# New priorities and re-measured costs in the list scheduler of a one-core encoder layer

## The chip, the core and the metric

The kernel runs on one core of one Trainium2 chip. The metric is the device time of one execution in microseconds (us); less is better. A core has five engines that run on their own and meet at semaphores: PE (TensorE, matrix products), DVE (VectorE), ACT (ScalarE), POOL (GpSimd) and SP (SyncE, which here only issues transfers). Each engine works off its own list of instructions strictly in the order in which the list was written: an instruction that has to wait holds up everything behind it on that engine.

## What is computed

The reference is one layer of a streaming encoder for 512 prompt frames and 32 sample frames (544 columns in all), cut here to its steps:

```python
xn = RMSNorm(x);  [q|k|v|iq|ik|iw|u|g_a|g_b] = xn @ w_in
score = sum_h iw[t,h] * relu(iq[t,h] . ik[s]);  top_idx = top_k(score, n_sel)
o_A = softmax(q . k[top_idx]) @ v[top_idx]          # sparse attention, GQA
m = u + (u_prev - u) * shift_mu                     # RWKV-7 branch, from u
S = S * w_t + (S @ a_t) b_t + v_t k_t;  y_t = S @ r_t
h = x + w_out(sigmoid(g_a) * (o_A @ w_oa) + sigmoid(g_b) * (y_B @ w_ob))
y = RMSNorm_final(h + SwiGLU(RMSNorm(h)))
```

All of it is in float32. A float32 product is done as three PE passes over operands that are split into a high and a low part.

## The kernel before

**Products.** `gemm` (line 279) multiplies one 128-column block of weights by the activations, in two halves of 272 columns, each in a PSUM bank of its own: 8 slices of the contraction by 3 passes are 24 matmuls per bank. Its weights come through `wblock`: a transfer (line 255) into `raw`, a rounding copy on ACT (line 256, the high part), a subtraction on DVE (line 260, the low part).

**The start.** `prologue` loads the input in eight slices (line 296, each 128x544), the first two blocks of w_x, small vectors and constants. Line 300 (ACT) and 301 (DVE) split every slice into `x0`, which the listings call `k`: x times the norm's gain, not yet divided by the root mean square. Three blocks are multiplied from `x0` directly (two of the low-rank part, group L, in banks 82 to 85, and the first block of group U0, in banks 86 and 89), 3 x 48 = 144 matmuls; line 758 scales their results afterwards. Meanwhile the sum of squares is made: lines 309, 311 (squares and sums), 316, 317 (twenty small matmuls), 318, 319, 322, then five transposes on PE (line 328), two copies on ACT (line 330), and from them, slice by slice, the normalised input `xn` (the listings' `r`): line 339 on DVE, 340 on ACT, 341 on DVE, eight times each. The next two blocks of U0 are multiplied from `xn` (2 x 48 = 96 matmuls), then line 392 makes keys and values. Lines 439 and 424, 425 load and split the first cached index keys, which nothing needs before the index scores much later.

**After that** the branches run interleaved: the index scores and the top-k search on DVE (lines 458, 459, 530, 604 to 616), attention, four pairs of RWKV heads with their preparation (lines 901 to 1045) and a recurrent chain of nine steps each (lines 1058, 1061, 1064 on PE, with copies on DVE, ACT and POOL between), the gates and the merge, all with blocks of line 279 between them as filler. From about 514 us on, gates, output projection and feed-forward are an unbroken sequence of large products (lines 279 and 1330).

**What sets the order.** The program is written once in the order of the string `ORDER`, whose words are groups (L, U0, KV, P0 ...). `plan` (line 1602) gives each instruction a priority: the one from the place where it is written, plus `SHIFT[group]`; the smaller goes first. `S` is the group of the sums of squares and of `xn`; a `w` ahead of a name means the group's weight blocks. `schedule` (line 1654) then walks through a model of the engines in time: whenever an engine is free it takes the ready instruction with the smallest priority. The model uses a duration per instruction (`cost`), a delay between engines (`HOP`), an extra for a change between partition halves (`TURN`) and a time for each transfer. Its only result is the order on each engine, which the program is then built with; nothing of the model's times goes to the chip.

## Time and profile before

| quantity | value |
|---|---|
| median of 3 runs | 1007.6 us (1006.28 to 1008.33) |
| the profiled execution, its own time | 1007.89 us |
| span of the profiled execution, first to last instruction | 1006.1 us |
| PE busy / DVE busy / ACT busy / POOL busy in the span | 964.9 / 628.1 / 460.0 / 190.4 us |
| mean granted TensorE clock | 0.985 |

The span leaves out 1.8 us of the profiled execution's own time that lie around it. A busy share is an average over stages with very different limits, so the rows further down split the span into stages.

### The profile page before, as it was taken

Reading aid. Unit: us, or ns where it says so; the run is one execution under the profiler, and the core shown is the slowest. Engines: PE = TensorE matmul, PEld = TensorE weight load, DVE = VectorE, ACT = ScalarE, POOL = GpSimd, SP = SyncE. Lnnn points to the kernel's source line nnn. Section 1 sums busy time; section 2 is a strip of 40 time slices with the busy share of each in tenths; the row PEclk is TensorE's granted clock in tenths of the full one; section 3 lists DMA queues with packets and bytes.
Section 4 is the critical chain, followed back from the end, with each engine's and each line's share of the span. In section 5 each row is a group of like instructions: output and inputs, shape, how many; then the busy total and the mean of one; then the engine's idle time right before and its main releaser. Section 6 shows DMA issues by size and latency. Waiting matters only on the chain.

```text
span 1006.1 us, 20829 instructions
## 1 busy us (share of the span) xinstructions
PE 964.9 (96%) x8268; PEld 923.4 (92%) x8268; DVE 628.1 (62%) x1452; ACT 460.0 (46%) x965; POOL 190.4 (19%) x307
## 2 busy tenths in 40 slices
PE   6989999999989999999999999999999999999996
PEld 5979997898879887899899999999999999999995
DVE  5947635999999898799677654444444444313132
ACT  6644555465546876565734452222323222223231
POOL 2212213322423421220000231111111111011112
PEclk9999999899999998999999999999999999999998
DMA  6246332432343455343555322232222233223222
GB/s 229 84 119 193 113 101 64 126 115 88 122 133 106 144 172 142 120 129 94 153 154 188 122 84 85 87 99 89 84 85 84 85 89 95 72 87 96 79 74 89
DMA packets 63282, 112.58 MB, mean 112 GB/s; under 512 B 13616, under 2 KB 33872, under 8 KB 63056
## 3 DMA queue, kind: packets, MB, share of 16 engines
q1 hardware_dynamic: 62144, 110.72, 35.7%
q8 instruction: 65, 1.06, 0.5%
q10 hardware_dynamic: 1040, 0.52, 0.2%
q14 instruction: 33, 0.27, 0.1%
HBM read 93.67 MB, written 17.14 MB: 110 GB/s over the span
## 4 chain that ended last, share of the span: by engine, by line
PE 72%; DVE 14%; DMA 6%; ACT 4%; issue 2%; SPq 1%; POOL 0%; DVEq 0%; ACTq 0%; POOLq 0%
PE bank L279 49%; PE bank L1330 13%; PE bank L458 1%; DVE w L260 1%; DVE f L616 1%; PE bank L459 1%; DMA iq_dram<-f 1%; DMA raw<-in_w_x_dram 1%; DVE f L611 1%; DVE f L615 1%; PE bank L901 1%; DVE f L529 1%; ACT w L256 1%; PE bank L1058 1%; DVE f L928 1%
## 5 line engine op out<-in xcount | busy, mean ns | idle before, releaser
L279 PE MATMUL bank<-r,w 128*128 128x272 f32 x4752 | 658.3, 293 | 3.2 <-ACT f L762 2.8
L279 PEld LDWEIGHTS bank<-r,w 128*128 128x128 f32 x4752 | 617.3, 189 | 10.0 <-ACT f L762 3.5
L256 ACT ACTIVATE w<-raw 128x1024 fp32r<-128x1024 f32 (+1 forms) x135 | 137.8, 1021 | 223.6 <-PE bank L279 172.7
L260 DVE TENSOR_TENSOR w<-raw,w 128x1024 fp32r<-128x1024 f32 (+1 forms) x135 | 176.5, 1308 | 97.8 <-ACT w L256 97.6
L1330 PE MATMUL bank<-r,w 128*128 128x272 f32 x1056 | 133.0, 288 | 0.0
L1330 PEld LDWEIGHTS bank<-r,w 128*128 128x128 f32 x1056 | 132.4, 188 | 0.0
L1308 POOL TENSOR_TENSOR f<-f 128x544 f32<-128x544 f32 x22 | 30.4, 1382 | 234.0 <-DVE f L1305 224.9
L1305 DVE TENSOR_TENSOR f<-bank,f 128x272 f32<-128x272 f32 x44 | 19.4, 442 | 74.8 <-PE bank L279 74.8
L1298 DVE TENSOR_TENSOR f<-bank,f 128x272 f32<-128x272 f32 x44 | 19.1, 435 | 45.1 <-PE bank L279 45.1
L453 POOL TENSOR_TENSOR k<-f,k 64x512 fp32r<-64x512 f32 (+1 forms) x22 | 30.1, 1372 | 49.0 <-ACT k L452 43.4
L458 PE MATMUL bank<-k 128*128 128x512 f32 (+5 forms) x102 | 35.8, 359 | 3.1 <-DVE f L645 1.3
L1332 DVE TENSOR_TENSOR f<-bank,f 128x272 f32<-128x272 f32 x16 | 7.1, 442 | 47.7 <-PE bank L1330 47.7
L1336 POOL TENSOR_TENSOR f<-f 128x272 f32<-128x272 f32 x13 | 12.4, 955 | 110.8 <-ACT f L1334 110.8
L459 PE MATMUL bank<-k 128*128 128x512 f32 (+5 forms) x102 | 33.0, 333 | 0.0
L1334 ACT ACTIVATE f<-f 128x272 f32<-128x272 f32 x16 | 6.8, 423 | 57.1 <-DVE f L1332 57.1
L1299 ACT ACTIVATE f<-f 128x272 f32<-128x272 f32 x44 | 18.7, 424 | 29.8 <-DVE f L1298 29.8
L611 DVE SCALAR_TENSOR_TENSOR f<-f,f 128x256 f32<-128x256 f32 (+2 forms) x45 | 31.7, 705 | 0.9 <-ACT f L604 0.3
L279 PE MATMUL bank<-k,w 128*128 128x272 f32 x144 | 22.8, 322 | 9.8 <-ACT k L300 9.8
L279 PEld LDWEIGHTS bank<-k,w 128*128 128x128 f32 x144 | 21.6, 219 | 10.1 <-ACT k L300 9.7
L458 PEld LDWEIGHTS bank<-k 128*128 128x128 f32 x102 | 19.1, 188 | 10.7 <-issue 5.1
L1074 POOL COPY f<-f 64x64 f32<-64x64 f32 x56 | 16.3, 292 | 65.3 <-DVE f L1071 63.9
L1250 POOL TENSOR_TENSOR f<-f 128x272 f32<-128x272 f32 x14 | 12.5, 896 | 75.3 <-DMA raw<-in_w_out_dram 51.7
(352 smaller groups left out, 1239.0 us busy)
## 6 DMA issues: line engine op xcount, KB each, us to landing
raw<-in_w_x_dram SPq DMA_DIRECT2D x41, 512.0 KB, 3.7
raw<-in_w_gate_dram SPq DMA_DIRECT2D x22, 512.0 KB, 3.6
raw<-in_w_up_dram SPq DMA_DIRECT2D x22, 512.0 KB, 3.6
raw<-in_w_down_dram SPq DMA_DIRECT2D x16, 512.0 KB, 3.6
gate_dram<-f SPq DMA_DIRECT2D x16, 272.0 KB, 2.4
raw<-in_w_oa_dram SPq DMA_DIRECT2D x8, 512.0 KB, 3.8
raw<-in_w_out_dram SPq DMA_DIRECT2D x8, 512.0 KB, 3.7
f<-iq_dram SPq DMA_DIRECT2D x26, 128.0 KB, 2.8
```

The source lines that it names most:

```text
L256: nc.scalar.activation(hi[:, a], raw[:, a], AF.Copy)
L260: self.lo_eng.tensor_tensor(lo[:, b], raw[:, b], hif[:, b], op=OP.subtract)
L279: nc.tensor.matmul(o, a[:, k], c[k][:, s], start=n == 0, stop=n == 3 * nk - 1)
L453: nc.gpsimd.tensor_tensor(ql[0:64], raw[0:64], qh_r.v(512)[0:64, :n], op=OP.subtract)
L458: nc.tensor.matmul(out, q[0][:, i:i + m], self.KS[:, j, keys], start=True, stop=False)
L459: nc.tensor.matmul(out, q[1][:, i:i + m], self.KS[:, j, keys], start=False, stop=stop)
L611: nc.vector.scalar_tensor_tensor(acc, r[:, i * S:(i + 1) * S], w, acc, op0=OP.mult, op1=OP.add)
L1298: nc.vector.tensor_tensor(t1[:, s], o, self.rs[:, s], op=OP.mult)
L1299: nc.scalar.activation(t1[:, s], t1[:, s], AF.Silu)
L1305: nc.vector.tensor_tensor(t2[:, s], o, self.rs[:, s], op=OP.mult)
L1308: nc.gpsimd.tensor_tensor(t1, t1, t2, op=OP.mult)
L1330: nc.tensor.matmul(o, a[:, k], c[k0 + k][:, s], start=m == 0, stop=m == 65)
```

## The change

The instructions stay the same, with the same operands and buffers (7,429 matmuls in both). What changes is the model and the table that decide the order. The delay from POOL to ACT goes from 250 to 112 ns and from POOL to DVE from 70 to 110 ns; ACT's turn goes from 128 to 132 ns. A transfer now occupies the queue of SP for 330 ns, or 585 ns where it covers fewer than 128 partitions (the new `narrow`), instead of 60 ns; its way through the queue is counted from that. All entries of `SHIFT` have new values.

```diff
 SHIFT = {
...
-    "R0": 299400, "R1": -1861400, "R2": -142400, "R3": 126400, "S": -59800, "SI": 126900, "U0": -21700, "U1": 1680300, "U2":
...
+    "R0": 156800, "R1": -241500, "R2": 188700, "R3": 345300, "S": -198800, "SI": -132300, "U0": -640200, "U1": 1595200,
...
-       ("Activation", "DVE"): 142, ("DVE", "Activation"): 128, ("DVE", "Pool"): 155, ("Activation", "Pool"): 210, ("Pool", "Activation"): 250,
-       ("Pool", "DVE"): 70, ("DVE", "DVE"): 127, ("Pool", "Pool"): 104, ("Activation", "Activation"): 60, ("PE", "PE"): 0}
+       ("Activation", "DVE"): 142, ("DVE", "Activation"): 128, ("DVE", "Pool"): 155, ("Activation", "Pool"): 210, ("Pool", "Activation"): 112,
+       ("Pool", "DVE"): 110, ("DVE", "DVE"): 127, ("Pool", "Pool"): 104, ("Activation", "Activation"): 60, ("PE", "PE"): 0}
...
-TURN = {"Activation": 128, "DVE": 110, "Pool": 112}
+TURN = {"Activation": 132, "DVE": 110, "Pool": 112}
...
+def narrow(i):
+
+    return any(list(x.ap)[0][1] < 128 for x in list(i.outs) + list(i.ins) if hasattr(x, "ap"))
...
-    sides = [0 if x or e in ("PE", "SP") else side(i) for x, e, i in zip(dma, engine, L)]
+    sides = [32 * narrow(i) if x else 0 if e == "PE" else side(i) for x, e, i in zip(dma, engine, L)]
...
                 if dma[k]:
-                    queue = max(t0 + 67, queue + 25) + 450
+                    issue = 585 if sides[k] else 330
+                    queue = max(t0 + 67, queue) + issue + 120
                     bus = max(queue + 650, bus) + work[k]
-                    end, free[e] = bus, t0 + 60
+                    end, free[e] = bus, t0 + (issue if e == "SP" else 60)
```

The order that comes out differs on every engine up to the long sequence of large products, and hardly in that sequence. Three places follow. In the listings a number behind `x` counts equal instructions in a row, and 128x272 is the size of the result.

**The first transfers**, on SP, in its queue's order from the first instruction. Before:

```order
L255 DMA raw<-in_w_x_dram 128x1024
L439 DMA f_74<-in_cache_keys_dram 128x512 x2
L225 DMA f_58<-in_vec_dram 128x80
L255 DMA raw<-in_w_x_dram 128x512
L296 DMA f_58<-in_x_t_dram 128x544 x4
L298 DMA f_58<-in_consts_dram 128x494
L255 DMA raw<-in_w_x_dram 128x512
L296 DMA f_58<-in_x_t_dram 128x544 x4
```

The same of the changed kernel:

```order
L255 DMA raw<-in_w_x_dram 128x1024
L225 DMA f_58<-in_vec_dram 128x80
L255 DMA raw<-in_w_x_dram 128x512
L296 DMA f_58<-in_x_t_dram 128x544 x4
L298 DMA f_58<-in_consts_dram 128x494
L255 DMA raw<-in_w_x_dram 128x512
L296 DMA f_58<-in_x_t_dram 128x544 x4
L439 DMA f_74<-in_cache_keys_dram 128x512 x2
```

The two transfers of cached keys (line 439) go from behind the first weight block to behind all eight slices of the input (line 296).

**The products around the transposes**, on PE, from the last small matmuls of the sum of squares on; `k` is `x0`, `r` is `xn`. Before:

```order
L279 MATMUL bank_83<-k,w 128x272 x5
L328 MATMUL bank_88<-f_58 128x32
L328 MATMUL bank_88<-f_58 128x128 x2
L328 MATMUL bank_87<-f_58 128x128 x2
L279 MATMUL bank_86<-k,w 128x272 x22
L279 MATMUL bank_89<-k,w 128x272 x22
L279 MATMUL bank_83<-k,w 128x272 x4
L279 MATMUL bank_84<-k,w 128x272 x11
L279 MATMUL bank_82<-r_70,w 128x272 x2
L279 MATMUL bank_85<-k,w 128x272 x14
L279 MATMUL bank_82<-r_70,w 128x272 x16
L279 MATMUL bank_85<-k,w 128x272 x5
```

The same place of the changed kernel:

```order
L328 MATMUL bank_88<-f_58 128x32
L279 MATMUL bank_86<-k,w 128x272 x22
L279 MATMUL bank_89<-k,w 128x272 x22
L328 MATMUL bank_88<-f_58 128x128 x2
L328 MATMUL bank_87<-f_58 128x128 x2
L279 MATMUL bank_82<-k,w 128x272 x2
L279 MATMUL bank_83<-k,w 128x272 x11
L279 MATMUL bank_84<-k,w 128x272 x11
L279 MATMUL bank_85<-k,w 128x272 x3
L279 MATMUL bank_82<-r_70,w 128x272 x2
L279 MATMUL bank_85<-k,w 128x272
L279 MATMUL bank_83<-r_70,w 128x272 x2
```

Before, all five transposes (line 328) stand ahead of the 44 products in banks 86 and 89; in the changed kernel four of them stand behind these 44. Counted from the first instruction, 65 products of `x0` stand ahead of the last transpose before (43 of them ahead of the small matmuls, 22 behind), and 107 in the changed kernel (50 and 57); 79 and 37 of the 144 stand behind it. Then come, in both kernels, the 96 products of `xn` up to the first product of line 392; in the changed kernel they change between banks 82 and 83 after one to five of them, and the last 48 of the 96 begin with the first one that uses the low part of the eighth slice of `xn`, which the eighth line 341 writes.

On DVE, the stretch that makes `xn`. Before, from the first line 339 on:

```order
L339 SCALAR_TENSOR_TENSOR f_58<-f_58 128x544 x2
L758 TENSOR_TENSOR f_58<-bank_82,f_58 128x272
L341 TENSOR_TENSOR r_70<-f_58,r_70 128x544 x2
L339 SCALAR_TENSOR_TENSOR f_58<-f_58 128x544 x2
L341 TENSOR_TENSOR r_70<-f_58,r_70 128x544 x2
L339 SCALAR_TENSOR_TENSOR f_58<-f_58 128x544 x2
L260 TENSOR_TENSOR w<-raw,w 128x1024
L341 TENSOR_TENSOR r_70<-f_58,r_70 128x544 x2
L339 SCALAR_TENSOR_TENSOR f_58<-f_58 128x544 x2
L758 TENSOR_TENSOR f_58<-bank_83,f_58 128x272
L341 TENSOR_TENSOR r_70<-f_58,r_70 128x544 x2
L758 TENSOR_TENSOR f_58<-bank_84,f_58 128x272
```

The changed kernel, from the same instruction on; after these rows come two more of line 758, the eighth line 339 and the second line 425, and the eighth line 341:

```order
L339 SCALAR_TENSOR_TENSOR f_58<-f_58 128x544 x2
L758 TENSOR_TENSOR f_58<-bank_82,f_58 128x272
L341 TENSOR_TENSOR r_70<-f_58,r_70 128x544
L758 TENSOR_TENSOR f_58<-bank_83,f_58 128x272
L339 SCALAR_TENSOR_TENSOR f_58<-f_58 128x544
L341 TENSOR_TENSOR r_70<-f_58,r_70 128x544
L260 TENSOR_TENSOR w<-raw,w 128x1024
L341 TENSOR_TENSOR r_70<-f_58,r_70 128x544
L339 SCALAR_TENSOR_TENSOR f_58<-f_58 128x544 x2
L260 TENSOR_TENSOR w<-raw,w 128x1024
L341 TENSOR_TENSOR r_70<-f_58,r_70 128x544 x2
L339 SCALAR_TENSOR_TENSOR f_58<-f_58 128x544 x2
```

From the first line 339 to the eighth line 341 there stand, besides the eight of each, two of line 758 and one of line 260 before, and three of line 758, two of line 260 and two of line 425 in the changed kernel.

**The end of a recurrent chain**, on PE, about 277 to 283 us of the trace before; the steps of the chain are lines 1058, 1061 and 1064. Before:

```order
L458 MATMUL bank_85<-k 128x128
L459 MATMUL bank_85<-k 128x128
L1058 MATMUL bank_89<-f_74 128x128
L458 MATMUL bank_84<-k 128x128
L459 MATMUL bank_84<-k 128x128
L1061 MATMUL bank_89<-f_58,f_74 128x64
L530 LDWEIGHTS f_74
L530 MATMUL bank_86<-f_74 128x2
L279 MATMUL bank_82<-r_70,w 128x272 x8
L1064 MATMUL bank_89<-f_74 128x128
```

The same step of the chain in the changed kernel, the last but one of its nine:

```order
L1058 MATMUL bank_89<-f_74 128x128
L279 MATMUL bank_83<-r_70,w 128x272 x8
L1061 MATMUL bank_89<-f_58,f_74 128x64
L279 MATMUL bank_83<-r_70,w 128x272 x8
L1064 MATMUL bank_89<-f_74 128x128
L279 MATMUL bank_83<-r_70,w 128x272
L530 LDWEIGHTS f_74
L530 MATMUL bank_86<-f_74 128x2
L279 MATMUL bank_83<-r_70,w 128x272 x2
L458 MATMUL bank_85<-k 128x128
L459 MATMUL bank_85<-k 128x128
```

Between lines 1058 and 1061 of this step stand two small matmuls of the scores (lines 458, 459) before, and eight products of line 279 in the changed kernel, where the scores come after the step. In the last step of the chain the products between 1058 and 1061 go from 8 to 11, and between 1061 and 1064 from 12 to 13. In the first step of the next chain (302 to 345 us of the trace before) it is the other way round: between 1058 and 1061 stood 13 products of line 279 and five other matmuls and now stand 2 products; from 1064 to the next 1058 there were 18 and now are 4.

## Rows read from the trace of the kernel before

**Rows 1.** Windows: length, PE, PEld, DVE, ACT, POOL busy, clock, DMA share, GB/s
```profile
9.75:24.60 14.85, 14.77 (x91) 14.26 (x91) 11.49 (x17) 10.57 (x17) 3.39 (x5) 0.89 0.59 208
24.60:46.70 22.10, 22.10 (x178) 22.04 (x175) 20.42 (x30) 14.24 (x25) 5.32 (x10) 1.00 0.28 79
46.70:75.00 28.30, 24.57 (x152) 23.46 (x150) 14.51 (x49) 13.70 (x39) 5.51 (x10) 0.94 0.41 121
75.00:160.00 85.00, 83.39 (x835) 77.43 (x833) 46.46 (x114) 46.01 (x109) 17.43 (x35) 1.00 0.42 128
160.00:225.00 65.00, 60.07 (x552) 54.53 (x551) 58.82 (x200) 38.11 (x95) 21.32 (x41) 0.95 0.33 103
225.00:302.00 77.00, 70.09 (x835) 63.33 (x835) 74.71 (x261) 40.72 (x103) 24.62 (x54) 1.00 0.37 117
302.00:345.00 43.00, 43.00 (x379) 39.34 (x373) 37.39 (x102) 31.38 (x85) 16.86 (x32) 1.00 0.43 136
345.00:514.00 169.00, 164.60 (x1425) 147.31 (x1424) 146.59 (x364) 109.78 (x256) 30.35 (x45) 0.98 0.44 133
514.00:988.80 474.80, 474.80 (x3792) 474.80 (x3791) 210.38 (x297) 148.32 (x230) 57.48 (x52) 1.00 0.31 94
```

**Rows 2.** Windows, same columns: the first transfers, and two clock dips
```profile
4.00:6.00 2.00, 0.00 (x0) 0.00 (x0) 0.56 (x1) 1.06 (x1) 0.69 (x1) 1.00 0.95 305
...
67.00:73.00 6.00, 6.00 (x34) 5.92 (x34) 2.81 (x11) 2.01 (x6) 2.48 (x2) 0.72 0.34 115
177.00:185.00 8.00, 5.80 (x25) 5.33 (x25) 7.14 (x20) 3.29 (x10) 4.42 (x9) 0.57 0.50 151
```

**Rows 3.** Timeline of SP's queue, 0 to 9 us
```profile
1.18 0.89 SPq L439 DMA_DIRECT2D f<-in_cache_keys_dram  x2
```

**Rows 4.** Timeline of PE, 17 to 47 us
```profile
19.58 4.44 PE L279 MATMUL bank<-k,w 128*128 128x272 f32 x22
23.95 0.88 PE L328 MATMUL bank<-f 32*128 32x32 f32 x5
24.58 7.65 PE L279 MATMUL bank<-k,w 128*128 128x272 f32 x59
...
36.98 9.87 PE L279 MATMUL bank<-r,w 128*128 128x272 f32 x77
46.72 0.58 PE L392 MATMUL bank<-w,r 128*128 128x336 f32 x2
```

**Rows 5.** DVE's groups, 25 to 50 us: busy and mean; idle before
```profile
L758 DVE TENSOR_TENSOR f<-bank,f 128x272 f32<-128x272 f32 x6 | 2.6, 435 | 0.0
L260 DVE TENSOR_TENSOR w<-raw,w 128x1024 fp32r<-128x1024 f32 x2 | 2.4, 1219 | 0.0
...
L425 DVE TENSOR_TENSOR k<-f,k 64x512 fp32r<-64x512 f32 x2 | 1.3, 686 | 0.0
```

**Rows 6.** Timeline of DVE, 16 to 40 us
```profile
25.37 1.48 DVE L339 SCALAR_TENSOR_TENSOR f<-f 128x544 f32<-128x544 f32 x2 [3.21 <-ACT f L330]
...
36.77 1.35 DVE L341 TENSOR_TENSOR r<-f,r 128x544 fp32r<-128x544 f32 x2
```

**Rows 7.** Timeline of PE, 62 to 68 us
```profile
66.75 0.33 PE L432 MATMUL bank<-f,f 128*128 128x128 f32 x1 [3.19 <-DVE f L406]
66.92 0.95 PE L1033 MATMUL bank<-f 128*128 128x2 f32 x8
```

**Rows 8.** PE's waits, 160 to 225 us: total, times, longest
```profile
PE bank L279 <- ACT f L762: 2.2, 1, 2.2
PE bank L1061 <- ACT f L1060: 1.6, 1, 1.6
```

**Rows 9.** PE's waits, 225 to 302 us
```profile
PE bank L530 <- DVE f L529: 1.7, 5, 0.5
PE bank L1061 <- ACT f L1060: 1.4, 3, 0.9
```

**Rows 10.** Timeline of PE, 277.5 to 283 us
```profile
279.49 0.43 PE L1061 MATMUL bank<-f,f 128*128 128x64 f32 x2 [0.92 <-ACT f L1060]
```

More of the change, by code (lines that the diff above doesn't have):

```diff
@@ L71 @@
 SHIFT = {
[7 rows of a table removed]
-    17100, "wstart": -230000,
[7 rows of a table added]
+    "wlate": 200900, "wstart": -163800,
 }
```

12 rows, old and new, of the table SHIFT are left out of this document.

## The prediction

> **What bounds the kernel now.** I read the profile in three passes: first a table of stages (how long, how much of it PE computes, how busy DVE is beside it, the granted clock), then, in every stage where PE stands still, its list of waits, and last the timelines at the places where the order changes. The reader is to see in the table [rows 1] that from 514 to 988.8 us PE is busy for 474.80 of 474.80 us. No order of instructions makes that shorter, and the order there hardly changes, so what the change does has to happen in the 514 us before. PE loses little there: after its first product at about 9.75 us it is idle 3.73 us of 46.7 to 75, 1.61 us of 75 to 160, 4.93 us of 160 to 225, 6.91 us of 225 to 302, nothing of 24.6 to 46.7 and of 302 to 345, and 4.40 us of 345 to 514 (stage length less PE's busy time, each). That is some 21.6 us, the stock from which a better order can save, besides the start. DVE shows where PE waits for data rather than for itself: 74.71 of 77 us busy from 225 to 302, 58.82 of 65 from 160 to 225, but only 14.51 of 28.3 from 46.7 to 75.
>
> The same table has the places where nothing is idle and something can be lost: from 24.6 to 46.7 us PE is busy for 22.10 of 22.10 us while DVE is busy for 20.42. The two run abreast, with no slack to spare on DVE.
>
> **The change, part by part.**
>
> *The start.* PE's first product waits for the first slice of the input. The queue is full: the first transfers keep the 16 DMA engines 0.95 busy at 305 GB/s [rows 2]. Moving the two transfers of cached keys behind the input takes 0.89 us out of SP's queue ahead of it [rows 3]; their bytes, 2 x 128 x 512 x 4 = 524 KB, take 524/305 = 1.7 us of a saturated bus. Lower bound of the gain 0.9, upper 1.7; as the bus is the fuller of the two I take 1.4 us, nearer the upper. What the keys feed (lines 424, 425) is late by that much and nobody waits for it early.
>
> *The transposes behind the 44 products.* This is the part that costs. Before, PE ends the last transpose at 24.58 us, when 65 products of `x0` are done; 59 more follow in one piece [rows 4], and DVE starts line 339 at 25.37, 0.79 us after the transposes [rows 6]. A product costs 9.87/77 = 0.128 us in the last of those pieces [rows 4]. In the new order 107 products stand ahead of the last transpose, 42 more: 42 x 0.128 = 5.4 us. So the transposes end at about 24.58 - 1.4 + 5.4 = 28.6, and the first line 339 starts at about 29.4. From there DVE needs longer too. Before, the first line 339 to the end of the eighth line 341 runs from 25.37 to 36.77 + 1.35 = 38.12, that is 12.75 us, back to back [rows 6]. In the new order one more line 758 (0.435), one more line 260 (1.219) and two of line 425 (0.686 each) stand between [rows 5], some 3.0 us: 15.8 us, so the eighth slice is ready at about 45.2. Behind it stand 48 products, 6.1 us, so line 392 starts at about 51.3, where it started at 46.72 [rows 4]. The cover that is gone are the 79 products of `x0` that used to stand behind the transposes while DVE made `xn`; 37 are left, 37 x 0.128 = 4.7 us, and with the 96 products of `xn` (12.3 us) PE has 17 us of work for the 22.7 us from 28.6 to 51.3. It stands idle for the difference, in small pieces.
> The net, with the gain of the start in it, is 51.3 - 46.72 = +4.6 us; I take **+4.5**, since neighbours on DVE overlap a little in their rows. Bounds: the dip of the clock that now lies in 9.75 to 24.6 (0.89 over 14.85 us, 1.6 us lost [rows 1]) may not come, +2.9; if PE's starved stretch lowers the clock for its 48 last products and some of line 392, up to +7.
>
> *The key products.* PE waits 3.19 us at line 432 for the norm of the index keys [rows 7]. The chain through ACT, DVE and POOL that makes it hangs on the products of line 392 just ahead and is not changed; a few small matmuls (line 1033) move ahead of the waiting one, out of a group of eight that takes 0.95 us [rows 7]: -0.4 us, for about half of them (0 to -0.95).
>
> *75 to 225 us.* From 75 to 160 the orders are nearly alike and there are 1.61 us to gain or lose: 0. From 160 to 225 the two big waits are for line 762 (2.2 us, the data of a block that comes back by a transfer) and for line 1060 (1.6 us, a chain step) [rows 8]; the operations ahead of both stand in the same order on ACT and SP: 0, with both ends at 2 us.
>
> *225 to 302 us.* PE waits for the top-k counts (line 529, 1.7 us in five pieces) and for the recurrent chain (line 1060, 1.4 us) [rows 9]. The longest of the chain's is the 0.92 us ahead of line 1061 [rows 10], where only two small score matmuls stand between it and line 1058; the new order has eight products there, 8 x 0.128 = 1.0 us, just what is missing. Most steps of this chain get eight to thirteen such products where they had two to twelve. But DVE is 97% busy, and what the chain's copies gain in line the top-k operations lose by some 5 us. So not all 6.91 us go: bounds 0 and -6.9, and I take half, -3.4.
>
> *302 to 345 us.* PE does not wait here now. The new order has two products where there were 13 and more ahead of line 1061 of the first step of the next chain, and four where there were 18 ahead of the second line 1058. Such a step has shown 0.92 us of wait with two small matmuls as cover [rows 10]; two or three new waits of that size less their cover are 0 to 3 us: +1.5.
>
> *345 us on.* The remaining 4.40 us are many small waits for the same chains: 0.
>
> The profiled execution took 1007.89 us, 0.3 above the median of 1007.6. Sum: 1007.9 + 4.5 - 0.4 - 3.4 + 1.5 = **1010.1 us**. Less than 0.2% of change, 1005.6 to 1009.6, is about what a measurement of this kernel cannot tell from none.
>
> **A row and a rule.** PE's clock falls where PE is busy in pieces: from 177 to 185 us it is busy 5.80 of 8 us and the granted clock is 0.57, which is mostly the lower of its two levels, 1.2 instead of 2.4 GHz; after the 3.19 us stop at 63.6 us, 67 to 73 us shows 0.72 [rows 2, 7]. The Trainium skill ("TensorE: Matmul & The Clock Gate", "HAM oscillation — how this bites in real kernels" and "A second HAM failure mode: psum-queue depth-cycling") says that waits between groups of matmuls, long ones or many short ones, send the clock back to half rate, so that what follows runs cold; the traces agree by these two rows. By that rule the starved stretch at 30 to 50 us, which did not exist before, costs more than its waits. From the rows: a dip like that of 67 to 73 loses 0.28 x 6 = 1.7 us, one like that of 177 to 185 0.43 x 8 = 3.4 us.
>
> **The rivals.** *Faster: the waits of 160 to 302 go.* They hold 4.93 + 6.91 = 11.8 us. For it speaks that DVE is the bound there, and that a different order of chain and top-k is all that it takes; also that a dip of the clock lies there. Against it: DVE's work is the same and leaves 2.3 us idle of 77. If 9 of the 11.8 us go instead of 3.4: 1010.1 - 5.6 = 1004.5. It decides from about 6 us on, where the sum falls to 1007.5. *Faster: the transposes don't hold DVE.* If PE reaches them earlier than worked out (products ahead of them at the better clock, or DVE's extra work in gaps that its rows don't show), the start's gain stays: 1007.9 - 1.4 - 0.4 - 3.4 + 1.5 = 1004.2. Against it speaks that both orders are fixed and that DVE was back to back already. *Slower still: the clock falls in the starved stretch*, +1.7 to +3.4, about 1012.5. *Nothing in the sum:* what is lost at 30 to 50 us is saved by 302, since DVE meanwhile gets ahead with line 425, 260 and 758 and the stages after are bound by DVE: 1007.6. Against it: DVE has 14 us of idle time just behind, so being ahead there is worth little.
>
> **How the numbers follow.** The forecast gets 0.44 (its own range 1008 to 1014); the first rival 0.18, the second 0.10, the clock 0.15, no change 0.13. Of the forecast's cases about a quarter lie below 1009.6 and a few below 1005.6; faster by over 0.2% is 0.18 + 0.10 and a little, together 0.29; slower is 0.15 and two thirds of 0.44, 0.44; the rest, 0.27, is within. The range from 1003.5 to 1015 leaves out the far ends of the first and the clock's rival.
>
> **What would show it.** Right: PE's first product at about 8.4 us; the last transpose at 28 to 29 us; DVE idle until then, and then back to back to about 45; PE idle for 5 to 7 us in many small pieces from 33 to 46, with DVE's line 341 as the releaser; line 392 from 50 to 52; PE idle for about 3.5 us from there to the place that is at 302 us now; some short waits of lines 1058 and 1061 behind it. Wrong: line 392 at or before 47 us, or a stage of 160 to 302 us with less than 4 us idle in all.

## The result, and the profile of the changed kernel

The changed kernel takes 1014.02 us (median of 5 runs, 1010.45 to 1015.15), the kernel before 1006.57 us in the same comparison (5 runs). The ratio is 1.0061 with a 95% interval of 1.0045 to 1.0076: slower by 0.6%. The profiled execution of the changed kernel took 1011.34 us, with a span of 1009.6 us (before: 1007.89 and 1006.1) and a mean granted clock of 0.985 in both. Of the five runs, the two with a granted clock of 0.985 took 1010.45 and 1011.34 us, the three with 0.974 to 0.981 took 1014.02 to 1015.15. The medians differ by 7.45 us. Of these, 3.45 us are the difference of the two profiled executions; 2.68 us are runs of the changed kernel with a lower clock than the one that was profiled, and 1.32 us come from a profiled execution before that was slower than the median of its five. Five runs of each are few: in the comparisons further down the kernel before took 1003.16 to 1016.78 us (35 runs). The ratios further down leave out the one execution (1024.54 us, with the changed start and the rest of before) that was over 1.5% above the fastest of its kernel.

First the windows of the changed kernel by stage (columns as in [rows 1]). From 52 us on they are cut about 5 us later than those of [rows 1]; from 76 to 240 us the changed kernel is only some 2 us late, as the table below them shows, so these stages are alike and not equal:

```profile
8.50:24.60 16.10, 15.82 (x94) 15.19 (x94) 11.26 (x17) 10.22 (x17) 4.00 (x5) 0.85 0.64 233
24.60:52.00 27.40, 23.45 (x166) 21.86 (x166) 20.99 (x32) 15.94 (x29) 8.41 (x11) 0.97 0.19 54
52.00:80.00 28.00, 25.78 (x174) 24.43 (x173) 16.87 (x53) 14.46 (x41) 5.64 (x10) 1.00 0.46 142
80.00:165.00 85.00, 84.31 (x845) 77.96 (x843) 46.30 (x116) 45.83 (x109) 17.03 (x37) 1.00 0.39 124
165.00:230.00 65.00, 59.34 (x593) 53.83 (x592) 59.57 (x206) 36.18 (x90) 20.63 (x39) 0.90 0.32 103
230.00:307.00 77.00, 74.21 (x850) 69.33 (x850) 70.93 (x251) 43.83 (x110) 26.49 (x54) 0.99 0.37 121
307.00:350.00 43.00, 39.49 (x282) 34.65 (x282) 37.28 (x103) 26.94 (x77) 17.84 (x30) 0.96 0.36 117
350.00:519.00 169.00, 164.57 (x1443) 146.85 (x1443) 145.88 (x362) 110.78 (x255) 33.15 (x44) 1.00 0.45 137
519.00:992.00 473.00, 473.00 (x3774) 472.84 (x3773) 209.46 (x297) 147.65 (x230) 57.15 (x51) 1.00 0.30 94
```

PE, which was never idle from 24.6 to 46.7 us, is now idle for 3.95 us from 24.6 to 52 us, and for 3.51 us from 307 to 350, where it was never idle either. From 52 to 80 us it is idle for 2.22 (before, the stage like it: 3.73), from 230 to 307 for 2.79 (before: 6.91). The sequence of large products is unchanged.

Where the two runs stand at the same instruction, by the start of that instruction in either trace:

| instruction on PE | before | changed | difference |
|---|---|---|---|
| first product | 9.75 | 8.19 | -1.56 |
| first of line 392 | 46.72 | 52.76 | +6.04 |
| first of line 826 | 73.61 | 76.21 | +2.60 |
| first of line 1058, second chain | 235.82 | 237.69 | +1.87 |
| last of line 530 (the sample's search) | 298.03 | 304.51 | +6.48 |
| first of line 1058, third chain | 311.61 | 313.14 | +1.53 |
| last of line 945 | 348.05 | 352.98 | +4.93 |
| first of line 1330 | 861.26 | 864.99 | +3.73 |

The loss is made in two places, before line 392 and from 305 to 350 us, and part of it comes back behind each.

Idle time of PE alone misleads here. These windows lie between the same instructions: from the first step of the second chain to that of the third, and from there to the last line 945. Before:

```profile
235.82:311.61 75.79, 69.81 (x749) 63.24 (x748) 72.86 (x243) 41.83 (x103) 26.69 (x57) 1.00 0.35 112
311.61:348.05 36.44, 36.44 (x290) 33.54 (x288) 31.72 (x86) 27.54 (x81) 15.10 (x30) 1.00 0.53 164
```

Changed:

```profile
237.69:313.14 75.45, 71.95 (x781) 67.33 (x781) 70.51 (x236) 41.08 (x104) 24.38 (x52) 1.00 0.37 119
313.14:352.98 39.84, 37.04 (x266) 32.33 (x264) 33.19 (x100) 28.36 (x82) 20.67 (x35) 0.96 0.41 128
```

In the first, PE's idle time falls from 5.98 to 3.50 us, but the stretch is only 0.34 us shorter, since PE does some 32 more matmuls in it. In the second these are missing: some 24 fewer, 2.80 us idle instead of none, and 3.40 us longer. The filler was brought forward, and most of the waits moved with it.

**The start.** PE's timeline of the changed kernel, which answers to [rows 4]:

```profile
8.19 8.58 PE L279 MATMUL bank<-k,w 128*128 128x272 f32 x50 [8.19 <-ACT k L300]
...
21.93 0.31 PE L328 MATMUL bank<-f 32*128 32x32 f32 x1
22.17 7.69 PE L279 MATMUL bank<-k,w 128*128 128x272 f32 x44
29.70 0.60 PE L328 MATMUL bank<-f 128*128 128x128 f32 x4
...
36.17 2.54 PE L279 MATMUL bank<-r,w 128*128 128x272 f32 x16 [0.72 <-DVE w L260]
39.98 1.52 PE L279 MATMUL bank<-r,w 128*128 128x272 f32 x10 [1.26 <-DVE r L341]
...
43.48 1.52 PE L279 MATMUL bank<-r,w 128*128 128x272 f32 x10 [0.97 <-DVE r L341]
...
52.76 3.54 PE L392 MATMUL bank<-w,r 128*128 128x336 f32 x22
```

The 44 products come between the first transpose and the other four; at 7.69/44 = 0.175 us each, as the clock is low there. The window of 18 to 27 us shows it (0.62), and three later ones show the starved stretch:

```profile
18.00:27.00 9.00, 8.72 (x46) 8.09 (x46) 1.86 (x3) 1.75 (x2) 1.19 (x1) 0.62 0.19 67
33.00:36.00 3.00, 2.46 (x20) 2.23 (x18) 3.00 (x5) 2.11 (x4) 0.34 (x1) 1.00 0.00 0
39.00:42.00 3.00, 1.52 (x11) 1.30 (x11) 2.97 (x6) 2.24 (x5) 1.61 (x1) 1.00 0.56 163
42.00:45.00 3.00, 2.03 (x12) 1.60 (x12) 2.94 (x5) 0.85 (x2) 0.82 (x3) 1.00 0.30 97
```

From 33 us on PE starves (busy 1.52 of 3 us at 39 to 42): 0.72 us for the low part of a weight block (line 260), the rest for the slices of `xn`. The granted clock stays at 1.00 there in this execution. DVE's timeline, which answers to [rows 6]:

```profile
30.84 1.48 DVE L339 SCALAR_TENSOR_TENSOR f<-f 128x544 f32<-128x544 f32 x2 [9.13 <-ACT f L330]
...
45.85 0.71 DVE L341 TENSOR_TENSOR r<-f,r 128x544 fp32r<-128x544 f32 x1
```

DVE waits 9.13 us for the transposes' copies and then works from 30.84 to 46.56 us: 15.72 us, where it took 12.75 us before.

**The stop at line 432** of [rows 7], 3.19 us, is down to parts of 0.8 and 0.9 us. PE's waits of the changed kernel, 52 to 80 us:

```profile
PE bank L432 <- ACT f L762: 0.9, 1, 0.9
PE bank L432 <- DVE f L406: 0.8, 1, 0.8
```

**305 to 320 us.** Two lines of DVE's timeline there:

```profile
308.68 2.33 DVE L573 TENSOR_TENSOR_SCAN f<-f 32x1056 f16<-32x1056 bf16 x1
...
311.33 1.30 DVE L574 SCALAR_TENSOR_TENSOR f<-f 32x1056 bf16<-32x1056 f16 x1
```

Two of ACT's:

```profile
313.88 0.40 ACT L1149 ACTIVATE f<-bank 128x272 f32<-128x272 f32 x1 [4.45 <-PE bank L279]
314.44 0.22 ACT L1060 ACTIVATE f<-bank 64x64 f32<-64x64 f32 x1 [0.17 <-DVE f L1059]
```

And two of PE's:

```profile
311.46 0.73 PE L1133 MATMUL bank<-f 128*128 128x272 f32 x2 [0.71 <-DVE f L1134]
...
314.71 0.43 PE L1061 MATMUL bank<-f 128*128 128x64 f32 x2 [0.87 <-ACT f L1060]
```

The last long operations of the sample's search (lines 573, 574) now run where lines 1129 and 1134 wait to go; line 1133 on PE waits 0.71 us for that. ACT stands 4.45 us before line 1149, a copy of a product's bank, and line 1060, which the chain needs, stands behind it; line 1061 waits 0.87 us.

### The profile page after: what moved, and what is told of

The parts are those of the page before. It is cut to its first block, busy times and chain, and to the rows that moved or that the text cites. A ratio compares the mean times of both kernels' runs of the same rounds, so it can differ in the third digit from the quotient of the medians.

```text
span 1009.6 us, 20834 instructions
## 1 busy us (share of the span) xinstructions
PE 968.1 (96%) x8268; PEld 924.5 (92%) x8268; DVE 626.4 (62%) x1452; ACT 459.4 (46%) x965; POOL 198.9 (20%) x307
## 4 chain that ended last, share of the span: by engine, by line
PE 68%; DVE 15%; DMA 5%; ACT 4%; issue 4%; POOL 2%; SPq 1%; DVEq 0%; ACTq 0%; POOLq 0%
PE bank L279 46%; PE bank L1330 13%; DVE w L260 2%; PE bank L458 2%; PE bank L459 1%; ACT w L256 1%; DVE f L616 1%; DMA raw<-in_w_x_dram 1%; DVE f L930 1%; DMA f<-o_dram 1%; DVE f L615 1%; PE bank L1064 1%; PE bank L1058 1%; DVE f L972 1%; DVE f L529 1%
## 5 line engine op out<-in xcount | busy, mean ns | idle before, releaser
L1074 POOL COPY f<-f 64x64 f32<-64x64 f32 x56 | 22.5, 402 | 69.7 <-DVE f L1071 67.7
L1299 ACT ACTIVATE f<-f 128x272 f32<-128x272 f32 x44 | 18.7, 424 | 29.8 <-DVE f L1298 29.8
```

The costliest lines, as they stand in the source:

```text
L1074: nc.gpsimd.tensor_copy(QH[ps, cc + 1, e], ZV[e][ps, cc + 1])
```

## The experiments

Each kernel below has the instructions of the two kernels in another order. `old` is the sequence in which the scheduler of before emitted them, `new` that of the changed kernel; a part of one up to a named instruction is followed by the rest of the other, on all engines at once:

```python
def upto(L, log, name):
    return log[:next(n for n, k in enumerate(log) if L[k].name == name)]

def join(head, tail, engine):
    first = set(head)
    order = {}
    for k in list(head) + [k for k in tail if k not in first]:
        order.setdefault(engine[k], []).append(k)
    return order
```

I-517 is the first product of line 392, I-2301 the sixth line 1058 of the first chain (164 us before), I-2999 the first line 1058 of the second (235.8 us), I-3134 the first line 1127 behind the second chain (304.8 us). The theory at the start: the transposes behind the 44 products make the loss, and the rest of the new order is worth something. The first rival: what comes after absorbs a late start, so that the loss has another place.

**The keys alone.**

```diff
-    return join(old, [], engine)
+    return join(late_keys(L, old), [], engine)      # line 439 behind the eighth line 296
```

> The order of before, with only the two transfers of cached keys (line 439) moved behind the eight slices of the input. Theory: the start is bound by the bus, the first product comes at 8.2 us instead of 9.75, and the whole time falls by 1.5 us (span near 1004.6). Rival: the gain is swallowed by the next wait (the weights of the first blocks, or the stop at line 432) and the time stays within 0.5 us of before.

Measured: ratio 1.000 (0.9976 to 1.0024); the profiled execution has its first product at 8.35 us, line 392 at 45.44 (-1.28), and a span of 1005.2 us. The start moved as expected, but a gain of 1.4 us is smaller than the interval. The theory is right on the place: the four traces with the keys ahead have the first product at 9.56 to 9.78 us. That line 392 follows isn't shown by one trace, since two traces with the whole start of before (of the kernel that changes at 235 us and of the one with the filler put back, both below) have it at 45.32 and 45.23 us without any key moved. Its worth in the time isn't shown either.

**The start of before, the rest changed.**

```diff
-    return join(new, [], engine)
+    return join(upto(L, late_keys(L, old), "I-517"), new, engine)
```

> Up to the first product of line 392 the order of before with the keys late, from there on the order of the changed kernel. Theory: the loss of the change is made by the transposes behind the 44 products alone, and what the changed kernel gives back from 48 us on (2.3 us of span) belongs to its order: line 392 at 45 us, span near 1002.3, 0.4% under before. Rival: what is given back between 48 and 80 us (3.4 us) is only the stop at line 432 getting shorter because everything is late; then the rest of the new order costs 1.1 us, span near 1005.7, and without the early loss the change is worth nothing.

Measured: ratio 1.0010 (0.9984 to 1.0036), span 1003.2 us, line 392 at 44.28, line 826 at 68.23 (5.38 ahead of before). PE's waits from 30 to 85 us:

```profile
PE bank L432 <- ACT f L762: 0.8, 1, 0.8
PE bank L392 <- DVE w L374: 0.7, 1, 0.7
PE bank L432 <- DVE f L406: 0.5, 2, 0.3
```

The stop of 3.19 us is down to 0.8 and 0.5 with a start that isn't late, so it is the new order that shortens it. It is not the count of products: by the timelines 96 of line 392 stand ahead of the waiting line 432 in both orders. What differs is SP's queue. The transfer that stores the first finished block of index keys (line 416) reads a buffer that line 398 writes again for the third block, and line 398 begins the norm that line 432 waits for. Before, four transfers of line 483 stand ahead of line 416, by SP's timeline:

```profile
57.61 2.60 SPq L483 DMA_DIRECT2D f<-f  x4
60.31 0.53 SPq L416 DMA_DIRECT2D out_idx_k_prompt_dram<-f  x1
```

In the run with only the keys moved, whose order here is that of before, DVE's timeline shows line 398 waiting for that very transfer:

```profile
62.10 0.22 DVE L398 COPY f<-bank 128x64 f32<-128x64 f32 x1 [1.68 <-DMA out_idx_k_prompt_dram<-f]
```

In the new order line 416 goes ahead of them, here at 54.12 us:

```profile
54.12 0.34 SPq L416 DMA_DIRECT2D out_idx_k_prompt_dram<-f  x1
```

Line 398 then starts at 58.63 us, 4.31 ahead of the waiting line 432 (before: 2.69), and 21 products of line 392 cover the norm. That is read from the traces; no run moves line 416 alone. Against the changed kernel's 1.0061 the time shows that the start makes most of the loss. The gain of the rest that the profile shows is not there in the medians; the rival's "worth nothing" fits those better, but its reason (the stop is short only because everything is late) is refuted.

**The changed start, the rest of before.**

```diff
-    return join(old, [], engine)
+    return join(upto(L, new, "I-517"), old, engine)
```

> Up to the first product of line 392 the order of the changed kernel, from there on that of before. Theory: line 392 starts 6 us late as in the changed kernel and nothing absorbs it, span near 1012, 0.6% over before. Rival (absorption): the stop at line 432 shrinks from 3.2 us to about 0 without any change in the order there, and the span is near 1008.7.

Measured: ratio 1.0053 (1.0027 to 1.0078): the start alone makes nearly the whole loss of 1.0061. The profiled execution is one of its fastest (1008.32 us), and in it the rival is seen at work: line 392 comes at 50.54, 3.82 us late, yet line 826 at 72.38, 1.23 us early. The stop at line 432 shrinks to 0.58 us in an order that didn't change, by PE's timeline:

```profile
67.07 0.33 PE L432 MATMUL bank<-f,f 128*128 128x128 f32 x1 [0.58 <-DVE f L406]
```

The transfer of line 416 lands within 1.8 us there (before, such transfers took up to 3.6), and line 398 waits only 0.27 us for it. Windows of that kernel at the 44 products, in the starved stretch and at this stop:

```profile
18.00:27.00 9.00, 8.09 (x61) 7.62 (x62) 1.48 (x3) 1.68 (x2) 1.71 (x2) 1.00 0.19 65
40.00:46.00 6.00, 5.28 (x28) 5.08 (x29) 5.96 (x11) 2.76 (x5) 1.64 (x4) 0.72 0.15 46
64.00:70.00 6.00, 5.42 (x39) 5.06 (x38) 3.56 (x18) 1.54 (x5) 1.62 (x2) 1.00 0.54 146
```

So in the trace a late start is absorbed there, and in the median of the runs it isn't. Here the clock does fall in the starved stretch (0.72 from 40 to 46 us), which it didn't in the trace of the changed kernel; in return it is 1.00 from 18 to 27 us, where that trace has 0.62. The order is the same up to line 392, so the 2.22 us between 50.54 and 52.76 are a spread of executions, with the clock's dip in another place.

**Before up to 235 us, then changed.**

```diff
+    return join(upto(L, old, "I-2999"), new, engine)
```

> Up to the first chain step of the second pair (line 1058, 235.8 us) the order of before, from there on the order of the changed kernel. Theory: behind that place the changed kernel is about neutral (it saves some 6 us of waits from 240 to 300 us, loses 8 us from 305 to 345 where the top-k search of the sample, put off by 6 us, meets the next chain, and saves 3 us after): span within 2 us of 1006. Rival: the loss at 305 to 345 us is a consequence of the late start and goes away with it: span near 1000.

Measured: ratio 1.0034 (1.0010 to 1.0058), span 1010.5 us. Ahead by 2.3 us at the second chain's first step (233.52), which is a spread of executions, as the order is that of before up to there; behind by 1.25 at the last line 945 and by 4.4 at line 1330. The changed order costs 0.3% from 235 us on, without any late start; both expectations (1006 and 1000 us) were too low.

**The transposes first.** On PE alone, in the changed kernel:

```diff
 L328 MATMUL bank_88<-f_58 128x32
-L279 MATMUL bank_86<-k,w 128x272 x22
-L279 MATMUL bank_89<-k,w 128x272 x22
 L328 MATMUL bank_88<-f_58 128x128 x2
 L328 MATMUL bank_87<-f_58 128x128 x2
 L279 MATMUL bank_82<-k,w 128x272 x2
 L279 MATMUL bank_83<-k,w 128x272 x11
+L279 MATMUL bank_86<-k,w 128x272 x22
+L279 MATMUL bank_89<-k,w 128x272 x22
```

> The changed kernel with one edit on PE alone: the 44 products of banks 86 and 89 move behind the last four transposes (line 328) and the 13 products that follow them. Theory (the place of these 44 makes the loss of the start): first line 339 at about 24.5 us instead of 30.8, PE does not starve between 33 and 46, line 392 at about 46 instead of 52.8, and the time falls by about 5 us to the level of the kernel whose start was that of before (within 0.3% of before). Rival (DVE's extra work of lines 260, 425 and 758 between the slices of xn, or the late start of another operand, makes it): line 392 comes at 50 us or later and the time stays over 1010.

Measured: ratio 1.0025 (1.0000 to 1.0049). Line 339 starts at 22.95 us, but line 392 only at 49.56, not at 46. ACT's timeline, where the next wait sits:

```profile
24.33 1.05 ACT L256 ACTIVATE w<-raw 128x1024 fp32r<-128x1024 f32 x1
...
33.00 1.06 ACT L256 ACTIVATE w<-raw 128x1024 fp32r<-128x1024 f32 x1 [5.85 <-PE bank L279]
```

The second weight copy (line 256) overwrites a buffer that the last products of `x0` read, waits 5.85 us for them, and holds up five of the eight lines 340. The ratio is less than half of the changed kernel's 0.6%, though the intervals overlap a little (up to 1.0049, from 1.0045). The edit met a second wait that the first had hidden.

**The same on three engines.**

```diff
 ACT
-L256 ACTIVATE w<-raw 128x1024
 L424 ACTIVATE k<-f_74 128x512 x2
...
 L340 ACTIVATE r_70<-f_58 128x544 x3
+L256 ACTIVATE w<-raw 128x1024
 DVE
 L339 SCALAR_TENSOR_TENSOR f_58<-f_58 128x544 x2
-L260 TENSOR_TENSOR w<-raw,w 128x1024
...
 L341 TENSOR_TENSOR r_70<-f_58,r_70 128x544
+L260 TENSOR_TENSOR w<-raw,w 128x1024
```

> The edit of the run with the transposes first, on three engines: besides the 44 products behind the transposes on PE, the second weight copy (line 256 on ACT) goes behind the eighth line 340 and its subtraction (line 260 on DVE) behind the eighth line 341, since ACT had stood 5.85 us ahead of that copy and held up the slices of xn. Theory: the start's loss is the sum of the two (transposes late, slices of xn queued behind a copy whose buffer is not free): line 392 at about 45 us and 0.3% less time than with the edit on PE alone, near the kernel that has the whole start of before. Rival: the two lines 425 and the third line 758 between the slices are enough to starve PE: line 392 at 48 us or later.

Measured: ratio 1.0052 (1.0025 to 1.0079), line 392 at 52.17. A miss. ACT again:

```profile
33.00 1.15 ACT L424 ACTIVATE k<-f 128x512 fp32r<-128x512 f32 x2 [6.05 <-PE bank L279]
```

Now the copies of the cached keys (line 424) wait 6.05 us at the same place, since their result lies in the memory of `x0`; before the change they stood behind all eight lines 340. And the weight copy, now late, holds up PE instead (line 260, 0.48 us). The expectation left out that line 424 stands ahead on ACT. The clock has a part in the 52.17 us, too:

```profile
39.00:51.00 12.00, 10.29 (x55) 9.48 (x56) 9.31 (x15) 5.97 (x11) 2.69 (x4) 0.72 0.34 96
```

The last 50 products ahead of line 392 take 8.71 us, 0.174 each; with the edit on PE alone, 54 took 7.41, 0.137 each. At that rate line 392 would come some 1.9 us earlier (an estimate), at 50 us: still a miss.

**The middle of the changed order.**

```diff
+    head = upto(L, late_keys(L, old), "I-517")
+    return join(head + [k for k in upto(L, new, "I-2999") if k not in set(head)], old, engine)
```

> Order of before with late keys up to the first product of line 392, order of the changed kernel from there to the first chain step of the second pair (line 1058, 235 us), order of before behind it. Theory: this keeps what the change gains (1.5 us at the start, 2 to 4 us from 48 to 235) and leaves out both losses (the transposes, and the stretch from 235 us on, which cost 3 us): 0.3 to 0.5% under before, about 1003 us. Rival: the gain from 48 to 235 us is lost again behind it, since the stages from 235 us on are set by DVE's work: within 0.2% of before.

Measured: ratio 0.9981 (0.9961 to 1.0001), 1005.66 us, span 1003.8. In the trace it is 3.8 us ahead at the first chain step (129.58) and 0.4 at the second chain's. The time is where the rival puts it. (The trace that changes at 235 us has that chain step at 130.50 in the order of before, so one trace tells little of these 3.8 us.)

> As the run with the middle of the changed order, but the order of before comes back at the sixth chain step of the first pair (164 us) and not at 235 us. Theory: the 4 us that are ahead at 164 us were lost from 170 to 240 us because the changed order there takes three waits for line 529 and a longer clock dip; with the order of before from there on they stay: 0.3 to 0.4% under before. Rival: DVE's work sets 164 to 345 us in either order: within 0.2% of before, no better than 1005.8 us.

With I-2301 in place of I-2999: ratio 0.9973 (0.9941 to 1.0006), 1004.87 us, span 1003.5 us. That lies between the theory (0.3 to 0.4% under before) and the rival (within 0.2%). Both are faster than the changed kernel, by intervals that don't meet; neither is separated from the kernel before.

**Before up to 304.8 us, then changed.**

```diff
+    return join(upto(L, old, "I-3134"), new, engine)
```

> Order of before up to line 1127 of the second pair (304.8 us), order of the changed kernel behind it. Theory: the 3 us that the changed order costs from 235 us on are made before 304 us, by putting off the sample's top-k search, whose last long operations on DVE (lines 571 to 575) then meet lines 1129 and 1134 and the next chain; with the search done in time the rest costs nothing: within 0.2% of before, and no wait of line 1133 for line 1134 over 0.3 us. Rival: it is the thin filler between the first steps of the next chain (2 products instead of 13): waits of lines 1061 and 1045 of 0.8 us each at 313 to 320 us stay, and the time is 0.2 to 0.4% over before.

Measured: ratio 1.0063 (1.0041 to 1.0086), span 1014.5. The theory falls: here the search has ended in time, and the loss is no smaller than with the changed order from 235 us on (1.0034; the intervals overlap). The rival is half right: line 1061 waits 0.73 us, but line 1045 does not wait, and the loss is larger than its 0.2 to 0.4%. Windows of 306 to 324 us:

```profile
306.00:312.00 6.00, 6.00 (x48) 5.84 (x48) 2.08 (x5) 2.02 (x4) 0.00 (x0) 1.00 0.30 94
312.00:318.00 6.00, 4.26 (x28) 3.63 (x27) 5.26 (x20) 3.50 (x9) 3.19 (x6) 0.90 0.25 96
318.00:324.00 6.00, 5.93 (x28) 5.52 (x28) 5.86 (x16) 3.78 (x14) 1.69 (x4) 0.53 0.25 89
```

PE is busy throughout from 306 to 312 us, while DVE (2.08 of 6 us) and ACT (2.02) wait for what stands behind PE's filler; then PE waits, and the clock falls to 0.53. The new order was laid out for a DVE that is busy with the search there, as in the changed kernel (6.00 of 6 us); where it isn't, PE's filler comes too early. That is the reading of this trace; the mixture stands in neither of the two kernels, so its 0.6% is not a price of the changed kernel's own stretch.

**The filler put back.** In that kernel, on PE:

```diff
 L1133 MATMUL bank_89<-f_58 128x272
-L279 MATMUL bank_83<-r_70,w 128x272 x9
+L279 MATMUL bank_83<-r_70,w 128x272 x2
 L1133 MATMUL bank_89<-f_58 128x272
-L279 MATMUL bank_83<-r_70,w 128x272 x9
-L1058 MATMUL bank_89<-f_58 128x128
-L279 MATMUL bank_83<-r_70,w 128x272 x2
+L279 MATMUL bank_83<-r_70,w 128x272 x5
+L1058 MATMUL bank_89<-f_58 128x128
+L279 MATMUL bank_83<-r_70,w 128x272 x13
 L1061 MATMUL bank_89<-f_58 128x64
```

(Two of line 826 and 827 move up with it.)

> The kernel with the order of before up to 304.8 us and the changed order behind it, with one edit on PE: the second line 1133 and the first line 1058 of the third chain move ahead of 13 of the 18 products that stood before them, and these 13 stand between lines 1058 and 1061, as before the change. Theory: there PE worked through its filler (6.00 of 6 us busy from 306 to 312) while DVE (2.08) and ACT (2.02) waited for it, and had none when the chain came; with the edit 2 to 4 us of the 7 lost by 340 us come back, time 0.2 to 0.4% under that kernel's 1015.1 us. Rival: the weights' copies and the score work behind it set the pace there: no change (within 1.5 us), new waits of lines 1064 and 1058.

Measured: ratio 1.0041 (1.0018 to 1.0065). That is 0.2% less, but the intervals overlap. The 13 products stand between the steps again, and line 1061 waits all the same, by PE's timeline:

```profile
311.64 1.87 PE L279 MATMUL bank<-r,w 128*128 128x272 f32 x13
314.25 0.44 PE L1061 MATMUL bank<-f 128*128 128x64 f32 x2 [0.73 <-ACT f L1060]
```

ACT's timeline at that time:

```profile
313.55 0.40 ACT L1149 ACTIVATE f<-bank 128x272 f32<-128x272 f32 x1 [4.24 <-PE bank L279]
313.98 0.22 ACT L1060 ACTIVATE f<-bank 64x64 f32<-64x64 f32 x1
```

On ACT line 1149 stands ahead of line 1060 and waits 4.24 us for the last of these very products. Before the change line 1060 stood ahead of it. So it isn't the count of products alone, but also the place of line 1149 on another engine. No run moves line 1149, so what its place costs in the time isn't shown.

**The two parts of the change apart.** The old table in the new model, and the new table in the old model:

> One part of the change alone: the new delays, turn and transfer times in the model with the old table of priorities. The start keeps the order of before (keys first, five transposes ahead of the 44 products). Theory (the loss comes from the table, through U0's and S's new entries): line 392 at 46 to 47.5 us, and a time within 0.3% of before. Rival (the new model itself orders worse): over 1011 us.

> The other part of the change alone: the new table of priorities in the old model. The transposes stand behind the 44 products as in the changed kernel. Theory (table and model fit only together, as the old table in the new model showed): 1% or more over before. Rival (the table alone makes the changed order): within 0.3% of the changed kernel's 1013 us.

Measured: ratios 1.0373 (1.0344 to 1.0403) and 1.0193 (1.0155 to 1.0232). Either part alone is far slower than both together, and neither is a near copy of one of the two kernels: from 160 to 345 us PE is idle for 21.05 us of 185 in the first and 16.36 in the second (before: 11.84, by [rows 1]). That is 9.2 and 4.5 us of spans that are 38.2 and 18.7 us longer; where the rest is lost was not followed up. The window of the old table in the new model:

```profile
160.00:345.00 185.00, 163.95 (x1613) 146.87 (x1613) 164.80 (x538) 100.04 (x258) 62.66 (x121) 0.94 0.33 101
```

And of the new table in the old model:

```profile
160.00:345.00 185.00, 168.64 (x1622) 148.88 (x1621) 163.61 (x538) 99.75 (x257) 65.49 (x121) 0.94 0.33 102
```

The theory for the first (the new entries of U0 and S make the loss, so the old ones don't) is wrong: the time is 3.7% over, and line 392 comes at 39.56 us, ahead of the 46 to 47.5 expected, in a start that is neither of the two. The theory for the second (1% or more) is right. Here either table did badly in the model that it doesn't belong to.

## Why the prediction came out as it did

The direction and the main mechanism were right: slower, by the late slices of `xn`. The median of 1014.02 us lies in the range, 3.9 us over the forecast of 1010.1; the profiled execution is 1.2 us over it. But that the sum came so near is in part luck: two of its terms were off by some 3 us each, in opposite directions. By the table of instructions:

| term | forecast | measured |
|---|---|---|
| the start, transposes and DVE, to line 392 | +4.5 | +6.04 |
| the key products, to line 826 | -0.4 | -3.44 |
| 75 to 225 us, to the second chain | 0 | -0.73 |
| 225 to 302 us, to the third chain | -3.4 | -0.34 |
| 302 to 345 us, to the last line 945 | +1.5 | +3.40 |
| 345 us on, to line 1330 | 0 | -1.20 |
| sum | +2.2 | +3.73 |

- *The start, -1.4:* measured -1.56. The keys alone give -1.40.
- *The transposes, net +4.5:* measured +6.04, inside the bounds. The steps are those of the prediction, 1.4 to 1.7 us later: transposes until 30.3 us instead of 28.6, because the 44 products ran at a low clock (0.175 us each, not 0.128); the first line 339 at 30.84 (29.4); DVE's run 15.72 us (15.8), back to back; line 392 at 52.76 (51.3). The other trace with this start has the clock at 1.00 there and +3.82, so the excess goes with the clock. PE was idle for 3.95 us, not 5 to 7, as the slow clock filled part of the gap. What the prediction didn't see lies one step behind: the two edits of the start show that with early transposes ACT stops until 33 us on line 256 or 424, which need the end of the products of `x0`, and line 392 still comes at 49.56 or later. What each of the three costs alone is not settled: they wait for the same products, and taking one away shows the next.
- *The key products, -0.4:* the term is mis-sized, and its reason was wrong. The prediction took the chain to line 432 as hanging on the products of line 392 and unchanged; it hung on a transfer in SP's queue (line 416 behind line 483), which the new order moves ahead, and the run with the start of before shows the stop at 0.5 to 0.8 us instead of 3.19. From the first line 392 to the first line 826 PE's idle time falls from 3.71 to 2.12 us, -1.6. About as much is clock: 0.94 over 26.89 us before, 1.00 now. That half need not belong to the order: the two kernels with the middle of the changed order have the same order there, and show 1.00 and 0.86 from 64 to 76 us.
- *75 to 225 us, 0:* -0.7, inside its 2 us.
- *225 to 302 us, -3.4:* the saving did not come, -0.3. PE's idle time did fall, by 2.5 us between the same instructions, but the prediction counted idle time that goes as time that is saved; PE filled it with products that were then missing in the next stretch. The other half of the sentence came true: the search is put off, its last line 530 comes 6.48 us late.
- *302 to 345 us, +1.5:* mis-sized, +3.4. Of that, 2.80 us are new waits, inside the bounds of 0 to 3, and some 1.7 us are the clock (0.72 from 318 to 324 us). The prediction priced thin filler by 0.92 us per step and left out what stands ahead on the other engines: DVE's search ahead of line 1134, line 1149 ahead of line 1060 on ACT. The run that begins the new order at 235 us puts all that follows there at 0.3%. Taken together, 225 to 345 us were to give 1.9 us back and cost 3.1.
- *345 us on, 0:* -1.2. The clock alone would give more: before it is 0.98 over 169 us there, some 3.4 us lost; now it is 1.00.

The runs of parts fit the whole within their intervals: the start alone costs 0.53%, the order from 235 us on 0.34%, the middle gives back 0.19% (with the keys late, which alone is 1.000): 0.68% against the measured 0.61%. So the start makes most of the loss; the part from 235 us on, for which the prediction had a gain, is a loss too.

The span grew by 3.5 us where the sum had 2.2. The rest of the measured 0.6% goes in part with the clock: the rival of the clock in the starved stretch did not happen in the profiled execution (1.00 from 33 to 45 us), but three of five runs had a lower clock than that one and took 1014 to 1015 us, and two of the kernels with a start like this show the dip right there (0.72 from 40 to 46 us in one of them, from 39 to 51 us in the other). The rule of the Trainium skill ("TensorE: Matmul & The Clock Gate", "HAM oscillation — how this bites in real kernels") that waits between groups of matmuls lead to half rate agrees with those, and is not borne out by the starved stretch of the changed kernel's own trace. That the lower clock of the three runs lies in this stretch isn't shown, since they have no trace. Nor is the mean clock all: the kernel with the changed start and the rest of before took 1008.32 and 1013.42 us in two executions with the same 0.987. Why its median lies 5 us over that of before, when its trace has most of the late start absorbed, stays open.

Of the rivals, the one that nothing in the sum remains (what is lost early is saved by 302 us) had the right kind of place: half of the early loss is back by line 826. It had the wrong reason, as the return comes at line 432 and in the clock behind it, and not from a DVE that is ahead.

## What to carry to other kernels

A list scheduler's table of priorities and its cost model belong together: with either changed alone, the time rose by 2 to 4% here. When an order starves an engine, read the in-order queue of every engine that feeds it, and ask for each instruction ahead of the needed one which buffer it waits for; that queue can be the one of the transfers, as at line 432. Moving one instruction on one engine uncovered the next such wait twice here. Idle time that goes from a busy engine is not time saved while the work that filled it is only brought forward: compare two traces between the same instructions. Work that covers a wait has to stand behind the instruction that starts the wait, and not ahead of it; the trace of the kernel that changes at 304 us suggests so (PE busy for 6.00 of 6 us, then for 4.26 of 6), while putting the filler back gave 0.2%, less than the intervals can tell.

## What was not expected of the hardware

The same program's granted clock differed from run to run, and the time with it: 0.974 to 0.985 and 1015.15 to 1010.45 us in the five runs of the changed kernel. One trace with a starved stretch (PE busy 1.52 of 3 us) kept the clock at 1.00, another with the same order there fell to 0.72. The first of them had its dip (0.62) from 18 to 27 us, the second none there, and they reached line 392 2.22 us apart. A difference of 1.5 us that one trace shows plainly (the keys alone) disappears in that.
